# The experts' loop of a two-layer encoder: the next tokens turned between the halves of a first product, the gated activations behind the second product

## The chip, the core and the metric

The kernel runs on one core of a Trainium2 chip. The core has five engines that run beside each other, each through its own queue in order: TensorE (PE, with its weight loads shown as PEld), VectorE (DVE), ScalarE (ACT), GpSimd (POOL) and SyncE (SP, which here only issues loads). The metric is the time of the whole program on the device in microseconds, the median of several runs.

## The reference

The program is an encoder of two layers over 1040 tokens (1024 and 16 learned ones) with 1024 columns. Each layer has a mixer (attention beside a linear recurrence), a layer norm, a mixture of experts, and a layer norm. This case is about the experts: each token is sent to two of 32, and an expert computes

```python
def expert_block(args):
    xe, e = args
    return (jax.nn.silu(xe @ w1[e]) * (xe @ w3[e])) @ w2[e]

yb = lax.map(expert_block, (xb, block_e)).reshape(n_rows, D)
y = jnp.zeros((T, D), jnp.float32).at[row_tok].add(yb.astype(jnp.float32) * row_gate[:, None])
```

`w1` and `w3` are 1024 x 256 each, `w2` is 256 x 1024, all of them float32.

## The kernel before

`moe_layer` (L1180) is called once a layer. It keeps 96 places (`CAP`) for each of the 32 experts (`NE`); what doesn't fit goes through a branch that runs only where an expert has more. Products are made of two parts a number: `high` (L1215, ACT) rounds a weight to the type that PE multiplies fast, `low` (L1219, DVE) takes what is left over, and `mm3` makes three matmuls of each product: high by high, high by low, low by high. `split` does the same for activations, its high part on ACT and its low part on DVE.

The 3 MB of an expert come as thirds (`raw`, 128 x 2048 each): two hold `w1` and `w3` side by side, one for each half of the 1024 rows, and the last holds `w2`. Six `raw` buffers stand in three pools. SP issues a load as soon as the buffer's last reader, a `low`, is done. `w` has six buffers of a high and a low part.

For an expert the loop does:

- `tokens` (L1284): POOL gathers 96 rows into `xs`, of which there are two.
- `turned` (L1230): PE transposes the rows in eight pieces into two `tp` tiles; ACT and DVE split them into `xT`.
- `first` (L1386), halves 0 and 1: 12 matmuls each of `xT` by a third of the weights into `ph`. All 24 go into one PSUM bank.
- `tanh` (L1395, ACT) and `gate` (L1399, two instructions on DVE) make the gated activations `th`.
- `upright` (L1253): PE transposes `th` in two pieces into one `tp` tile; ACT and DVE split it into `aT`.
- `product` (L1261): 12 matmuls by the last third into `py`, two PSUM banks.
- `stored` (L1269): ACT scales `py` by the tokens' gates in two halves into `y`, and POOL scatters its rows (L1273).

`tp` has two buffers, taken in turn by the two tiles of `turned` and the one of `upright`. In PSUM, `tp`, `ph` and `py` fill all eight banks.

The loop runs under `manual_schedule`, so each engine's queue holds the instructions in the order of the code. Round e turns the activations of e, makes the first product of e + 1 and the second of e, prepares the weights of e + 2, turns the tokens of e + 2, and asks for the tokens and the weights of e + 4. The mixers outside are ordered by a scheduler that sees the whole program.

Of the kernel before, what the change touches and what calls it, by code (L numbers as in the profile page):

```python
# [11 lines left out]
F32 = mybir.dt.float32  # L12
# [3 lines left out]
AF = mybir.ActivationFunctionType  # L16
# [5 lines left out]
DEPTH, D, SEQ, META = 2, 1024, 1024, 16  # L22
# [12 lines left out]
NE = 32  # L35
EMPTY = 8192
CAP = 96
# [103 lines left out]
def pool(tc, **kw):  # L141
    return tc.tile_pool(reuse_waits="tile", **kw)
# [12 lines left out]
def pair(pool, shape, name, **kw):  # L155
    return Pair(pool.tile(shape, F32R, name=name + "_hi", **kw), pool.tile(shape, F32R, name=name + "_lo", **kw))
# [14 lines left out]
def hybrid_encoder(ctx: ExitStack, tc: tile.TileContext, I, out):  # L171
# [184 lines left out]
    for li in range(DEPTH):  # L356
# [650 lines left out]
        with mix, ExitStack() as late, pool(tc, name="opp", bufs=2, space=PSUM) as pp, \  # L1007
# [14 lines left out]
            for q, (i, n, col) in enumerate(tiles):  # L1022
# [38 lines left out]
                if len(batch) == size:  # L1061
                    route(op_, batch, lg, lambda: pt_.tile([128, 512], F32, name="pt"))
                    batch = []
            route.tables(op_)
        moe_layer(tc, I, li, last, K, split, mm3, moe, rt, route, h_rows[2 * li + 1], y_dst, nt, dram)
        moe.close()
    combine(DEPTH - 1, None, None)
# [112 lines left out]
def moe_layer(tc, I, li, last, K, split, mm3, stack, rt, route, h1_rows, y_rows, nt, dram):  # L1180
    nc = tc.nc
    ident = K("ident")
    n_rows = nt * 128 if last else L
    V = nc.vector
    VS, XS, GS, M, rk, cnt = route.VS, route.XS, route.at[:, 1], route.M, route.rk, route.cnt
# [4 lines left out]
    def space(name, bufs=1):  # L1190
        return stack.enter_context(pool(tc, name=name + str(li), bufs=bufs))
# [3 lines left out]
    wk, ra = space("moa", 2), space("mob", 2)  # L1195
    wx, ov = space("mox", 2), space("ov")
    rc, ww, rb = (stack.enter_context(pool(tc, name=f"mo{x}{li}", bufs=k, side="right"))
                  for x, k in (("c", 2), ("w", 6), ("d", 2)))
    with pool(tc, name="mop", bufs=1, space=PSUM) as pp:
        xs = [wk.tile([128, D], F32, name=f"xs{q}", bufs=1) for q in range(2)]  # L1200
# [4 lines left out]
        def loaded(src, spaces=(ra, rc, rb)):  # L1205

            r = []
            for q in range(3):
                raw = spaces[thirds[0] // 2 % len(spaces)].tile([128, 2048], F32, name="raw")
                thirds[0] += 1  # L1210
                nc.sync.dma_start(raw, src(q))
                r.append(raw)
            return r

        def high(raw, w, c):  # L1215
            cs = slice(c * 512, (c + 1) * 512)
            nc.scalar.activation(w.hi[:, cs], raw[:, cs], AF.Copy)  # L1217

        def low(raw, w, c):  # L1219
            cs = slice(c * 512, (c + 1) * 512)  # L1220
            V.tensor_tensor(w.lo[:, cs], raw[:, cs], w.hi[:, cs].bitcast(F32), op=OP.subtract)  # L1221

        def third(raw):
            w = pair(ww, [128, 2048], "w")
            for c in range(4):
                high(raw, w, c)
                low(raw, w, c)
            return w

        def turned(x, n):  # L1230
            xT = pair(wx, [128, 8, 128], "xT")[:, :, :n]
            for q in range(2):
                tp = pp.tile([128, 4, 128], F32, name="tp", bufs=2)
                for c in range(4):
                    nc.tensor.transpose(tp[:, c, :n], x[:n, (4 * q + c) * 128:(4 * q + c + 1) * 128], ident[:n, :n])
                split(xT[:, 4 * q:4 * q + 4], tp[:, :, :n])
            return xT
# [15 lines left out]
        def upright(th, n):  # L1253
            tp = pp.tile([128, 4, 128], F32, name="tp", bufs=2)
            for c in range(2):
                nc.tensor.transpose(tp[:, c, :n], th[:, c * 128:(c + 1) * 128], ident[:n, :n])
            aT = pair(wx, [128, 2, 128], "aT")[:, :, :n]
            split(aT, tp[:, 0:2, :n])
            return aT

        def product(aT, w, n):  # L1261
            py = pp.tile([128, D], F32, name="py", bufs=2)
            for j in range(2):
                for c in range(2):
                    mm3(py[:n, j * 512:(j + 1) * 512], aT[:, c], w[:, c * D + j * 512:c * D + (j + 1) * 512],
                        start=c == 0, stop=c == 1)
            return py

        def stored(py, n, vs, gs, rows):  # L1269
            y = wk.tile([128, D], F32, name="y")  # L1270
            for j in range(2):
                nc.scalar.activation(y[:n, j * 512:(j + 1) * 512], py[:n, j * 512:(j + 1) * 512], AF.Copy, scale=gs)  # L1272
            nc.gpsimd.indirect_dma_start(out=rows, out_offset=bass.IndirectOffsetOnAxis(ap=vs, axis=0), in_=y[:n],  # L1273
                                         in_offset=None, bounds_check=2 * n_rows - 1, oob_is_err=False)

        def gather(x, src, xi, rows):
            return nc.gpsimd.indirect_dma_start(out=x, out_offset=None, in_=src[:],
                                                in_offset=bass.IndirectOffsetOnAxis(ap=xi, axis=0),
                                                bounds_check=rows - 1, oob_is_err=False)

        def of(e):
            return loaded(lambda q: I["w_moe"][li, e, :, q * 2048:(q + 1) * 2048])

        def tokens(e):  # L1284
            return gather(xs[e % 2][:CAP], h1_rows, XS[:CAP, e:e + 1], n_rows)


        views = dram_disjoint_views(y_rows[:], NE)
# [85 lines left out]
        raws = [of(0), of(1)]  # L1374
# [4 lines left out]
        with tc.issue_after(route.act.ins), tc.issue_after(route.dve.ins), tc.issue_after(known.ins), tc.issue_after(second.ins):  # L1379
            ws = {0: [third(raws[0][q]) for q in range(2)]}  # L1380
# [3 lines left out]
        phs, ths, xTs = {}, {}, {}  # L1384

        def first(e, half):  # L1386
            if half == 0:
                phs[e] = pp.tile([128, 512], F32, name="ph", bufs=2)
            hidden(phs[e], ws[e][half], xTs[e], CAP, half)

        def portion(e, q):
            if e < NE:
                ws.setdefault(e, []).append(third(raws[e][q]))

        def tanh(e):  # L1395
            ths[e] = wk.tile([128, 256], F32, name="th")[:CAP]
            nc.scalar.activation(ths[e], phs[e][:CAP, :256], AF.Tanh, scale=0.5)

        def gate(e):  # L1399
            th, ph = ths[e], phs.pop(e)  # L1400
            V.scalar_tensor_tensor(th, th, 1.0, ph[:CAP, :256], op0=OP.add, op1=OP.mult)
            V.scalar_tensor_tensor(th, th, 0.5, ph[:CAP, 256:], op0=OP.mult, op1=OP.mult)

        with tc.manual_schedule():
            xTs[0] = turned(xs[0], CAP)
            first(0, 0)
            tokens(2)
            first(0, 1)
            tanh(0)
            gate(0)  # L1410
            xTs[1] = turned(xs[1], CAP)
            tokens(3)
            portion(0, 2)
            raws.append(of(2))
            for q in range(3):
                portion(1, q)
            raws.append(of(3))
            for e in range(NE):
                more, new = e + 1 < NE, e + 2 < NE
                aT = upright(ths.pop(e), CAP)  # L1420
                if more:
                    first(e + 1, 0)
                portion(e + 2, 0)
                if more:
                    first(e + 1, 1)
                portion(e + 2, 1)
                if new:
                    raw, w = raws[e + 2][2], pair(ww, [128, 2048], "w")
                    ws[e + 2].append(w)
                    high(raw, w, 0)  # L1430
                if more:
                    tanh(e + 1)
                    gate(e + 1)
                py = product(aT, ws.pop(e)[2], CAP)
                if new:
                    for c in range(4):
                        if c:
                            high(raw, w, c)
                        low(raw, w, c)
                    if e + 4 < NE:  # L1440
                        raws.append(of(e + 4))
                stored(py, CAP, VS[:CAP, e:e + 1], GS[:CAP, e:e + 1], views[e])
                if new:
                    xTs[e + 2] = turned(xs[e % 2], CAP)
                    if e + 4 < NE:
                        tokens(e + 4)


def rwkv(tc, li, last, K, P, pc, kr_d, bk_d, bon_d, g_dram, vt_d, yT, mhalf, kept, side, ready):
# [326 lines left out]
```

## Time and profile before

| what | value |
|---|---|
| median of 3 runs | 3237.86 us (3231.32 to 3243.92) |
| profiled execution, its own time | 3243.99 us |
| span of the profiled execution | 3242.1 us |
| PE busy | 2737.0 us, 84% |
| DVE busy | 2174.9 us, 67% |
| ACT busy | 1658.0 us, 51% |
| POOL busy | 1040.8 us, 32% |
| low parts of the experts' weights, DVE L1221 | 768, 472.8 us |
| high parts of the experts' weights, ACT L1217 | 768, 412.1 us |

The expert loops are the two stretches in which the memory queues are at nine tenths in the page's second part: about 1223 to 1580 us and 2821 to 3184 us of the span. A busy share over the whole span says little about them; what an expert costs is read inside these stretches. In rows of a timeline the first number is the start, the second the time until the last of the merged instructions ends, and in brackets stands the idle time before with what ended it. An instruction's time there includes what the next one overlaps, so where many follow each other their cost is the distance of the starts.

### The profile page before, as it was taken

The numbers are of one execution on the slowest core, as the hardware profiler recorded it, in microseconds if no ns is written. First come the engines' busy times: TensorE is split into PE (matmuls) and PEld (weight loads), VectorE is DVE, ScalarE is ACT, GpSimd is POOL, SyncE is SP. The second block draws the span as 40 slices with busy tenths as digits, with TensorE's granted clock in tenths as the row PEclk, the third lists the DMA queues.
The fourth block names the chain that finished last, engine by engine and source line by source line (L and its number), as shares of the span: only waits on it lengthen the run. The fifth ranks groups of instructions, "written<-read, shape, count | busy, mean of one in ns | idle before, by whom it ended". The sixth has DMA issues, their size and how long they took to land. (4 is left out here: it accounts for less than half of the span.)

```text
span 3242.1 us, 57910 instructions
## 1 busy us (share of the span) xinstructions
PE 2737.0 (84%) x22160; PEld 2231.9 (69%) x22160; DVE 2174.9 (67%) x4257; ACT 1658.0 (51%) x3604; POOL 1040.8 (32%) x1049
## 2 busy tenths in 40 slices
PE   5989899979998978888498997999699889788882
PEld 4878687768776765666388876888587767566551
DVE  7667554566677668888656747445666666787885
ACT  5334454544445447777433435445344434577772
POOL 3656211143336411111245632112433544111111
PEclk9999899968978979999799988988787879799996
DMA  5345610233323449999724565102432325688875
GB/s 175 103 144 174 200 35 21 66 108 105 91 78 96 144 176 327 323 318 314 252 70 136 161 205 182 40 14 75 130 101 67 95 81 185 235 310 313 309 278 223
DMA packets 342732, 523.76 MB, mean 162 GB/s; under 512 B 110733, under 2 KB 263309, under 8 KB 315809
## 3 DMA queue, kind: packets, MB, share of 16 engines
q1 hardware_dynamic: 234832, 399.11, 38.2%
q10 hardware_dynamic: 93280, 87.04, 7.9%
q0 software_dynamic: 14336, 33.84, 2.9%
q8 instruction: 176, 2.88, 0.4%
q14 instruction: 108, 0.88, 0.1%
HBM read 406.57 MB, written 129.84 MB: 165 GB/s over the span
## 5 line engine op out<-in xcount | busy, mean ns | idle before, releaser
L1221 DVE TENSOR_TENSOR w_lo<-raw,w_hi 128x512 fp32r<-128x512 f32 x768 | 472.8, 684 | 9.3 <-ACT w_hi L1217 9.1
L1217 ACT ACTIVATE w_hi<-raw 128x512 fp32r<-128x512 f32 x768 | 412.1, 620 | 0.0
L201 PE MATMUL pj<-hT_hi,w_hi 128*128 128x352 f32 (+1 forms) x912 | 303.3, 333 | 3.7 <-ACT k L437 2.7
L202 PE MATMUL pj<-hT_lo,w_hi 128*128 128x352 f32 (+1 forms) x912 | 301.4, 331 | 2.8 <-DVE hT_lo L212 2.8
L203 PE MATMUL pj<-hT_hi,w_lo 128*128 128x352 f32 (+1 forms) x912 | 299.7, 329 | 0.0
L1273 POOL DMA_INDIRECT y_rows<-y,VS x64 | 64.5, 1007 | 617.6 <-ACT y L1272 595.7
L201 PE MATMUL ph<-w_hi,xT_hi 128*96 128x512 f32 x512 | 226.9, 443 | 3.4 <-ACT w_hi L1217 3.4
L202 PE MATMUL ph<-w_lo,xT_hi 128*96 128x512 f32 x512 | 222.7, 435 | 1.3 <-DVE w_lo L1221 1.3
L203 PE MATMUL ph<-w_hi,xT_lo 128*96 128x512 f32 x512 | 221.4, 432 | 0.0
L1509 PE MATMUL e<-T,BK 64*128 64x128 f32 x1072 | 171.8, 340 | 38.3 <-DMA T<-kr_d 21.0
L212 DVE TENSOR_TENSOR pT_lo<-tr,pT_hi 128x512 fp32r<-128x512 f32 (+2 forms) x176 | 101.4, 592 | 127.5 <-ACT pT_hi L209 127.0
L201 PEld LDWEIGHTS pj<-hT_hi,w_hi 128*128 128x128 f32 x912 | 176.6, 194 | 14.6 <-issue 6.9
L202 PEld LDWEIGHTS pj<-hT_lo,w_hi 128*128 128x128 f32 x912 | 176.6, 194 | 9.3 <-issue 4.9
L1509 PEld LDWEIGHTS e<-T,BK 64*128 64x128 f32 x1072 | 145.0, 234 | 54.1 <-ACT AA L1515 19.8
L203 PEld LDWEIGHTS pj<-hT_hi,w_lo 128*128 128x128 f32 x912 | 176.1, 193 | 5.0 <-issue 4.3
L1514 DVE TENSOR_TENSOR T<-e,cc 64x512 f32<-64x512 f32 x134 | 92.2, 688 | 89.3 <-PE e L1509 86.9
L1654 POOL TENSOR_TENSOR sp<-ring,pc 64x256 f32<-64x256 f32 x126 | 85.2, 676 | 165.9 <-DVE ring L1667 145.1
L209 ACT ACTIVATE pT_hi<-tr 128x512 fp32r<-128x512 f32 (+2 forms) x176 | 86.7, 517 | 94.3 <-PE tr L873 92.9
L1551 DVE TENSOR_TENSOR sb<-sb,dg 128x16 f32<-128x16 f32 (+8 forms) x270 | 107.1, 397 | 40.5 <-POOL dg L1543 33.4
L203 PEld LDWEIGHTS ph<-w_hi,xT_lo 128*96 128x96 f32 x512 | 93.1, 182 | 43.1 <-issue 3.2
L201 PEld LDWEIGHTS ph<-w_hi,xT_hi 128*96 128x96 f32 x512 | 93.4, 182 | 42.5 <-ACT w_hi L1217 4.1
L202 PEld LDWEIGHTS ph<-w_lo,xT_hi 128*96 128x96 f32 x512 | 93.1, 182 | 40.2 <-DVE w_lo L1221 2.3
(422 smaller groups left out, 7635.3 us busy)
## 6 DMA issues: line engine op xcount, KB each, us to landing
raw<-in_w_moe_dram SPq DMA_DIRECT2D x192, 1024.0 KB
w_raw<-in_w_in_dram SPq DMA_DIRECT2D x38, 512.0 KB
T<-kr_d SPq DMA_DIRECT2D x134, 128.0 KB
ys<-y_rows SPq DMA_DIRECT2D x16, 1024.0 KB
a_d<-ht SPq DMA_DIRECT2D x25, 512.0 KB
h_rows<-h ACTq DMA_DIRECT2D x24, 512.0 KB
kr_d<-KR ACTq DMA_DIRECT2D x16, 576.0 KB
bk_d<-BK ACTq DMA_DIRECT2D x16, 576.0 KB
```

Of the source, the lines that this page charges most:

```text
L201: nc.tensor.matmul(o, a.hi, b.hi, start=start, stop=False)
L202: nc.tensor.matmul(o, a.hi, b.lo, start=False, stop=False)
L203: nc.tensor.matmul(o, a.lo, b.hi, start=False, stop=stop)
L209: hi = nc.scalar.activation(dst.hi, src, AF.Copy)
L212: return hi, e_lo.tensor_tensor(dst.lo, src, dst.hi.bitcast(F32), op=OP.subtract)
L1217: nc.scalar.activation(w.hi[:, cs], raw[:, cs], AF.Copy)
L1221: V.tensor_tensor(w.lo[:, cs], raw[:, cs], w.hi[:, cs].bitcast(F32), op=OP.subtract)
L1273: nc.gpsimd.indirect_dma_start(out=rows, out_offset=bass.IndirectOffsetOnAxis(ap=vs, axis=0), in_=y[:n], in_offset=None, bounds_check=2 * ...
L1509: nc.tensor.matmul(ps[o][:, u], BK[h, q0 + u].rearrange("p a t -> p (a t)"), T[h, q0 + u, o], start=True, stop=True)
L1514: V.tensor_tensor(T[b, q, o], ps[o][b], mask[b, None, :].to_broadcast([64, 4, 128]), op=OP.mult)
L1551: V.tensor_tensor(sb[:, :, cs], sb[:, :, cs], dg[:, :, t_:t_ + 1].to_broadcast([128, n, w]), op=OP.mult)
L1654: nc.gpsimd.tensor_tensor(sp[a], ring[a, :, o], pc[a, d, :, c:c + 1].to_broadcast([64, 4, 64]), op=OP.mult)
```

## The change

The arithmetic, the tiles and the buffers stay as they are. In a round of the loop three things move:

- `turned` for e + 2, with its gather for e + 4, moves from the end of the round to between the two halves of the first product of e + 1.
- `upright` for e + 1 moves from the start of the next round to directly behind the second product of e. On ACT its high part stands between the two halves of the scaling.
- The weights of e + 2 are prepared in a finer order: the first third at the start, the middle third behind `turned` with its last low part after the gate, the first two pieces of `w2` before the scaling, the last two after it.

The scaling gets its own helper, `scaled`, and the scatter stands in the loop.

```diff
+        def scaled(y, py, e, j):
+            nc.scalar.activation(y[:CAP, j * 512:(j + 1) * 512], py[:CAP, j * 512:(j + 1) * 512], AF.Copy,
+                                 scale=GS[:CAP, e:e + 1])
+
         with tc.manual_schedule():
...
+            aT = upright(ths.pop(0), CAP)
             for q in range(3):
                 portion(1, q)
             raws.append(of(3))
             for e in range(NE):
                 more, new = e + 1 < NE, e + 2 < NE
-                aT = upright(ths.pop(e), CAP)
                 if more:
                     first(e + 1, 0)
                 portion(e + 2, 0)
+                if new:
+
+                    xTs[e + 2] = turned(xs[e % 2], CAP)
+                    if e + 4 < NE:
+                        tokens(e + 4)
                 if more:
                     first(e + 1, 1)
-                portion(e + 2, 1)
                 if new:
-                    raw, w = raws[e + 2][2], pair(ww, [128, 2048], "w")
-                    ws[e + 2].append(w)
-                    high(raw, w, 0)
+                    mid, w1 = raws[e + 2][1], pair(ww, [128, 2048], "w")
+                    ws[e + 2].append(w1)
+                    for c in range(4):
+                        high(mid, w1, c)
+                        if c < 3:
+                            low(mid, w1, c)
                 if more:
                     tanh(e + 1)
                     gate(e + 1)
                 py = product(aT, ws.pop(e)[2], CAP)
+                y = wk.tile([128, D], F32, name="y")
                 if new:
-                    for c in range(4):
-                        if c:
-                            high(raw, w, c)
+                    low(mid, w1, 3)
+                    raw, w = raws[e + 2][2], pair(ww, [128, 2048], "w")
+                    ws[e + 2].append(w)
+                    for c in range(2):
+                        high(raw, w, c)
+                        low(raw, w, c)
+                scaled(y, py, e, 0)
+                if more:
+                    aT = upright(ths.pop(e + 1), CAP)
+                scaled(y, py, e, 1)
+                nc.gpsimd.indirect_dma_start(out=views[e], out_offset=bass.IndirectOffsetOnAxis(ap=VS[:CAP, e:e + 1], axis=0),
+                                             in_=y[:CAP], in_offset=None, bounds_check=2 * n_rows - 1, oob_is_err=False)
+                if new:
+                    for c in range(2, 4):
+                        high(raw, w, c)
                         low(raw, w, c)
                     if e + 4 < NE:
                         raws.append(of(e + 4))
-                stored(py, CAP, VS[:CAP, e:e + 1], GS[:CAP, e:e + 1], views[e])
-                if new:
-                    xTs[e + 2] = turned(xs[e % 2], CAP)
-                    if e + 4 < NE:
-                        tokens(e + 4)
```

The order in which the instructions stand shows the move on three engines. First PE, before, at the end of a second product in the middle of the loop (`py` is the second product, `xs` the tokens, `th` the gated activations, `ph` the first product):

```order
L201 MATMUL py<-w_hi,aT_hi 96x512
L202 MATMUL py<-w_lo,aT_hi 96x512
L203 MATMUL py<-w_hi,aT_lo 96x512
L1235 MATMUL tp<-cc,xs_12507 128x96 x8
L1256 MATMUL tp<-cc,th 128x96 x2
```

PE of the changed kernel, in the middle of a first product:

```order
L201 MATMUL ph<-w_hi,xT_hi 96x512
L202 MATMUL ph<-w_lo,xT_hi 96x512
L203 MATMUL ph<-w_hi,xT_lo 96x512
L1235 MATMUL tp<-cc,xs_12507 128x96 x8
L201 MATMUL ph<-w_hi,xT_hi 96x512
L202 MATMUL ph<-w_lo,xT_hi 96x512
L203 MATMUL ph<-w_hi,xT_lo 96x512
```

The eight transposes of the tokens have moved between matmuls of the first product, and the two of the activations follow the second product alone.

ACT before, one round from `tanh` to `tanh`:

```order
L1397 ACTIVATE th<-ph 96x256
L1217 ACTIVATE w_hi<-raw 128x512 x3
L1272 ACTIVATE y<-py,at 96x512 x2
L209 ACTIVATE xT_hi<-tp 128x4x96 x2
L209 ACTIVATE aT_hi<-tp 128x2x96
L1217 ACTIVATE w_hi<-raw 128x512 x9
```

ACT of the changed kernel, one round:

```order
L1397 ACTIVATE th<-ph 96x256
L1217 ACTIVATE w_hi<-raw 128x512 x2
L1405 ACTIVATE y<-py,at 96x512
L209 ACTIVATE aT_hi<-tp 128x2x96
L1405 ACTIVATE y<-py,at 96x512
L1217 ACTIVATE w_hi<-raw 128x512 x6
L209 ACTIVATE xT_hi<-tp 128x4x96 x2
L1217 ACTIVATE w_hi<-raw 128x512 x4
```

The high part of the activations has moved between the two scalings, and that of the tokens away from them, between weights.

DVE before, one round from the gate to the next:

```order
L1401 SCALAR_TENSOR_TENSOR th<-th,ph 96x256
L1402 SCALAR_TENSOR_TENSOR th<-th,ph 96x256
L1221 TENSOR_TENSOR w_lo<-raw,w_hi 128x512 x4
L212 TENSOR_TENSOR xT_lo<-tp,xT_hi 128x4x96 x2
L212 TENSOR_TENSOR aT_lo<-tp,aT_hi 128x2x96
L1221 TENSOR_TENSOR w_lo<-raw,w_hi 128x512 x8
```

DVE of the changed kernel, one round:

```order
L1401 SCALAR_TENSOR_TENSOR th<-th,ph 96x256
L1402 SCALAR_TENSOR_TENSOR th<-th,ph 96x256
L1221 TENSOR_TENSOR w_lo<-raw,w_hi 128x512 x3
L212 TENSOR_TENSOR aT_lo<-tp,aT_hi 128x2x96
L1221 TENSOR_TENSOR w_lo<-raw,w_hi 128x512 x6
L212 TENSOR_TENSOR xT_lo<-tp,xT_hi 128x4x96 x2
L1221 TENSOR_TENSOR w_lo<-raw,w_hi 128x512 x3
```

The tokens' low parts now stand in the middle of the weights, and three low parts of the middle third stand between them and the gate.

## The prediction

> **What bounds the kernel now.** The page's slices show two stretches of five slices with the memory queues at nine tenths; they are the two expert loops. I therefore read POOL's timeline first: POOL sends each expert's result away (L1273), so the starts of these rows are the loop's clock. First, thirtieth, thirty-first and last expert of layer 0, then of layer 1:
>
> ```profile
> 1223.23 3.22 POOL L1273 DMA_INDIRECT y_rows<-y,VS  x1 [15.87 <-ACT y L1272]
> ...
> 1564.67 0.93 POOL L1273 DMA_INDIRECT y_rows<-y,VS  x1 [11.63 <-ACT y L1272]
> 1575.70 0.91 POOL L1273 DMA_INDIRECT y_rows<-y,VS  x1 [10.11 <-ACT aT_hi L209]
> 1580.34 0.91 POOL L1273 DMA_INDIRECT y_rows<-y,VS  x1 [3.72 <-ACT y L1272]
> ...
> 2821.29 3.24 POOL L1273 DMA_INDIRECT y_rows<-y,VS  x1 [15.86 <-ACT y L1272]
> ...
> 3166.74 0.93 POOL L1273 DMA_INDIRECT y_rows<-y,VS  x1 [10.17 <-ACT y L1272]
> 3179.43 0.91 POOL L1273 DMA_INDIRECT y_rows<-y,VS  x1 [11.76 <-ACT aT_hi L209]
> 3184.07 0.91 POOL L1273 DMA_INDIRECT y_rows<-y,VS  x1 [3.73 <-ACT y L1272]
> ```
>
> From first to thirtieth are 29 steps: 341.44 us in layer 0 (1564.67 - 1223.23) and 345.45 us in layer 1. The 58 steps take 686.9 us, 11.84 each. What an expert needs of each engine stands in the view by windows; the first row covers 26 experts, the next two one expert each:
>
> ```profile
> 1249.00:1552.00 303.00, 260.06 (x1196) 183.25 (x1196) 247.79 (x442) 232.99 (x469) 49.51 (x52) 0.94 0.91 316
> ...
> 1237.96:1248.95 10.99, 9.33 (x46) 6.65 (x46) 9.53 (x17) 8.97 (x20) 1.91 (x3) 1.00 0.93 307
> 1248.95:1261.52 12.57, 10.91 (x46) 7.61 (x46) 9.53 (x17) 8.97 (x20) 1.91 (x3) 0.86 0.92 329
> ```
>
> Columns: stretch, its length, then PE, PEld, DVE, ACT, POOL busy, granted clock, memory queues' share, GB/s. 303 / 26 = 11.65 us an expert, while PE needs 9.33 at full clock, DVE 9.53 and ACT 8.97. No engine is full, so waits set the pace. An expert takes 10.99 us at clock 1.00, or 12.57 when a half-clock stretch falls in: 1.58 more. The list of waits for the same 303 us names the wait on PE, and one expert on PE shows where it lies:
>
> ```profile
> PE tp L1256 <- DVE xT_lo L212: 43.1, 26, 1.7
> ...
> 1285.82 0.38 PE L1256 MATMUL tp<-cc,th 96*128 96x96 f32 x2 [1.66 <-DVE xT_lo L212]
> 1285.99 0.46 PE L201 MATMUL ph<-w_hi,xT_hi 128*96 128x512 f32 x1
> ...
> 1291.57 0.39 PE L201 MATMUL py<-w_hi,aT_hi 128*96 128x512 f32 x1
> ...
> 1294.33 0.82 PE L1235 MATMUL tp<-cc,xs 96*128 96x96 f32 x8
> ...
> 1296.81 0.39 PE L1256 MATMUL tp<-cc,th 96*128 96x96 f32 x2 [1.66 <-DVE xT_lo L212]
> 1296.98 0.46 PE L201 MATMUL ph<-w_hi,xT_hi 128*96 128x512 f32 x1
> ```
>
> PE's order is: turn the gated activations (`upright`, 0.17 us to the next row), 24 matmuls of the first product (5.58), 12 of the second (2.76), turn the next tokens (`turned`, 0.82), and wait 1.66. The wait is for a PSUM buffer: `tp` has two, `turned` fills both, and `upright` can have one only when ACT and DVE have split it. ACT does this last, behind two `y` scalings that themselves wait for the second product.
>
> The half-clock stretches hang on the same place. The same view for the `ph` matmuls alone, cut into 3.41 us pieces:
>
> ```profile
> 1294.49:1297.90 3.41, 0.92 (x4) 0.73 (x5) 0.00 (x0) 0.00 (x0) 1.00 0.93 356
> 1297.90:1301.31 3.41, 3.41 (x9) 2.22 (x8) 0.00 (x0) 0.00 (x0) 0.50 0.83 285
> 1318.38:1321.79 3.41, 1.25 (x6) 0.93 (x7) 0.00 (x0) 0.00 (x0) 1.00 0.99 384
> 1321.79:1325.20 3.41, 3.41 (x16) 2.39 (x15) 0.00 (x0) 0.00 (x0) 1.00 0.84 317
> ```
>
> A piece with 0.92 us of product matmuls is followed by a piece at clock 0.50; one with 1.25 us is not. The stretch without them (1294.33 to 1296.98, 2.65 us, transposes included) costs 1.66 in every expert, and another 1.58 in those where nearly all of it falls into one piece.
>
> **The change, step by step.** It removes and adds no arithmetic; only orders move. Durations on ACT and DVE come from these rows, one expert of ACT, and a run of DVE at the loop's start in which it never pauses:
>
> ```profile
> 1286.24 0.33 ACT L209 ACTIVATE aT_hi<-tp 128x192 fp32r<-128x192 f32 x1 [0.69 <-PE tp L1256]
> 1286.47 4.79 ACT L1217 ACTIVATE w_hi<-raw 128x512 fp32r<-128x512 f32 x9
> 1294.53 1.26 ACT L1272 ACTIVATE y<-py,at 96x512 f32<-96x512 f32 x2 [0.82 <-PE py L203]
> 1295.69 0.86 ACT L209 ACTIVATE xT_hi<-tp 128x384 fp32r<-128x384 f32 x2
> ...
> 1287.12 4.91 DVE L1221 TENSOR_TENSOR w_lo<-raw,w_hi 128x512 fp32r<-128x512 f32 x8 [0.16 <-ACT w_hi L1217]
> ...
> 1217.27 0.35 DVE L212 TENSOR_TENSOR aT_lo<-tp,aT_hi 128x192 fp32r<-128x192 f32 x1
> 1217.54 4.89 DVE L1221 TENSOR_TENSOR w_lo<-raw,w_hi 128x512 fp32r<-128x512 f32 x8
> 1222.36 0.41 DVE L1401 SCALAR_TENSOR_TENSOR th<-th,ph 96x256 f32<-96x256 f32 x1
> 1222.80 0.42 DVE L1402 SCALAR_TENSOR_TENSOR th<-th,ph 96x256 f32<-96x256 f32 x1
> 1223.13 2.49 DVE L1221 TENSOR_TENSOR w_lo<-raw,w_hi 128x512 fp32r<-128x512 f32 x4
> 1225.54 1.01 DVE L212 TENSOR_TENSOR xT_lo<-tp,xT_hi 128x384 fp32r<-128x384 f32 x2
> ```
>
> *PE.* `turned` now stands between the halves of the first product, `upright` right behind the second. PE alone: 0.17 + 5.58 + 0.82 + 2.76 = 9.33 us an expert. `upright` now waits for two things: its `tp` buffer, whose reader finished half an expert ago, and the gate on DVE. The second tile of `turned` needs the buffer of the last `upright`, asked for 3.4 us after that (0.17 + 2.8 + 0.4); DVE reaches `aT_lo` about 2 us after it (below). Neither stalls PE.
>
> *The circle of waits.* Put `upright` at 0. The second product ends at 9.33. ACT starts `y` 0.20 later (1294.33 to 1294.53), at 9.53; a scaling takes 0.58 (two to the next row: 1.16), so `aT_hi` starts at 10.11, the second `y` at 10.33 (0.23 later), the third high part of w2 at 10.91. Its low part on DVE starts 0.65 later (1286.47 to 1287.12), at 11.56. Behind it DVE has six low parts at 0.60 (4.82 for eight, 1217.54 to 1222.36), two `xT_lo` (1.01), three low parts of the middle third (1.81) and the gate (0.86, 1222.36 to 1223.22): 7.30 us, to 18.86. The next but one `upright` follows, say at 18.9. That is two periods: 9.45 us each. Ahead of that low part DVE does one middle part, two w2 parts and `aT_lo`, some 2.4 us from the gate, which just fits.
>
> *DVE and ACT.* DVE's whole work for an expert, without a pause, is 9.28 us by the run above (1217.27 to 1226.55). ACT needs 8.97. Both lie below 9.45.
>
> *The token fetch.* POOL's gather for e+4 moves ahead of the store of y(e); it starts when `turned` is done, some 6 us earlier in the expert, and its data are wanted almost two experts later. Nothing queues behind it but that store. Cost: nothing. *SP* still issues three loads an expert, each when DVE frees a buffer.
>
> *Clock.* Without the 1.66 wait no 3.41 us piece holds more than about 0.82 + 0.17 + 0.1 us without product matmuls, far from the 2.5 of the piece above. The half clock should go from the loop.
>
> *Memory.* An expert moves 316 GB/s x 303 us / 26 = 3.68 MB. Two stretches of 20 us at the loops' starts hold the same mix, with DVE nearly always busy (19.2 of 20 us), and one of 7 us only weights:
>
> ```profile
> 1215.00:1222.00 7.00, 7.00 (x34) 4.89 (x33) 7.00 (x13) 7.00 (x16) 0.00 (x0) 0.93 1.01 425
> 1212.00:1232.00 20.00, 15.97 (x61) 10.95 (x61) 19.27 (x35) 16.71 (x34) 4.20 (x2) 0.82 0.99 385
> 2810.50:2830.50 20.00, 15.77 (x63) 10.86 (x63) 19.23 (x35) 16.27 (x34) 4.22 (x2) 0.84 0.99 382
> ```
>
> 3.68 MB at 383 GB/s is 9.6 us. The bounds: 9.45 by the circle if the queues do better, and 10.6 if the 303 us are the measure (316 GB/s at a share of 0.91 is 347 at 1.00; 3.68 / 0.347). The Trainium skill ("DMA: Bandwidth & Descriptors", Where 436 GB/s comes from) speaks against the change here: it puts what one core gets from its memory at about 358 GB/s, by which an expert could not go below 10.3 us. The 425 and 385 above, of a core alone on its chip, disagree. I take **9.6 us**, the value of the rows with the same mix.
>
> *Start and end.* The store of y(0) now waits for `upright(1)`, which stands behind `xT_lo` on DVE: about 2 us later. The two last experts turn no tokens. The thirtieth to thirty-first step becomes 0.17 + 5.58 + 2.76 = 8.5 us; the last about 3.8 (now 4.64, less the `aT_hi` that no longer waits for both `y`). Together 12.3 for 15.67 and 17.33.
>
> *The rest.* The second layer's mixer (1585 to 2757) is ordered by a scheduler and comes out slightly rearranged. I take nothing, with 17 us to both sides: so much do the two layers' stages ahead of the experts differ.
>
> ```profile
> 1585.00:2757.00 1172.00, 1015.96 (x9251) 868.10 (x9252) 730.05 (x1400) 508.95 (x1135) 445.42 (x447) 0.86 0.38 116
> 0.00:1155.00 1155.00, 1015.47 (x9570) 860.65 (x9571) 746.97 (x1453) 534.32 (x1203) 448.72 (x460) 0.91 0.37 112
> ```
>
> *Sum.* Layer 0: 341.4 - 29 x 9.6 - 2 = 61.0, end 3.4. Layer 1: 345.45 - 278.4 - 2 = 65.0, end 5.0. Together 134 us. The profiled execution took 3243.99 us, so 3110 by it; the median of three was 6.1 lower, 3237.86, so **3104 us** against that.
>
> **The rivals.**
>
> *Memory sets the pace at 10.6 us.* For it: a share of 0.91 over 303 us, with bursts of weights, stores and gathers on the same queues. Against it: the 385 and 382. 58 x 1.0 = 58 us more: 3162. By the page's 358 GB/s (10.3 us) it would be 3144. Chance 0.17.
>
> *The half clock stays, whatever the gap.* Then each expert keeps the mean loss of 0.65 (11.65 - 11.0): 9.6 + 0.65 = 10.25, 38 us more: 3142. Against it: the four pieces above. The Trainium skill ("TensorE: Matmul & The Clock Gate", Why this matters for your kernels) warns only of idle gaps over about 3 us between bursts; by that rule the gap of 2.65 costs no clock today, and its going saves none. The rows disagree: the clock fell behind a piece with 2.49 us free of products. Its Part 4 says that transposes do not count as busy, and the rows agree: only so do 0.92 and 1.25 part the two cases. Chance 0.08.
>
> *The wait only moves.* The gate comes late on DVE by what was won, since three low parts and two `xT_lo` stand ahead of it, and `upright` waits 1.66 and more as before: 3238. From the circle I get under 0.1 us of wait. Chance 0.03.
>
> *Slower: a late gate that also costs the clock.* If the middle third of the weights lands late, ACT holds `tanh` behind it, and `upright` waits. From a wait of about 2.3 us on (2.49 less 0.17) the piece falls under 0.92 us of products again. An expert then takes 9.33 + 2.3 + 0.65 = 12.28, 0.44 over 11.84: 58 x 0.44 = 26 us, 3263. Against it: the high parts, which read `raw`, had no idle time before any of the 768. Chance 0.04.
>
> ```profile
> L1217 ACT ACTIVATE w_hi<-raw 128x512 fp32r<-128x512 f32 x768 | 412.1, 620 | 0.0
> ```
>
> **How the numbers follow.** My forecast (9.4 to 9.9 us an expert, mixer as now) has 0.68. Its likeliest time is 3104. The low end is 9.45 an expert (58 x 0.15 = 9 less) and a mixer faster by about 15: 3080. The high end takes in memory at 10.6 with 8 for the mixer: 3170. Faster by over 0.5% (under 3222, about what a measurement of this kernel can tell from no change): 0.68 + 0.17 + 0.08 = 0.93. Within: 0.03. Slower: 0.04.
>
> **What would show it.** POOL's stores 9.4 to 9.9 us apart, without the 11.0 and 12.6; PE's wait ahead of `upright` under 0.3 us; clock 1.00 throughout the loops; about 380 GB/s there. If ACT's high parts wait for `raw`, memory is the bound. If clock 0.5 pieces remain, the second rival holds. If the 1585 to 2757 stage moves by over 17 us, the scheduler's part is mis-sized.

## The result, and the profile after

The changed kernel takes 3147.85 us (median of 4 runs, 3129.36 to 3161.33), the kernel before 3240.89 us beside it (4 runs, 3231.32 to 3247.85): a ratio of 0.971, 95% interval 0.966 to 0.975. In a second series (run e1 below) it was 0.972, 0.968 to 0.977. The direction and the range of the prediction hold. Its gain of 134 us does not: the medians differ by 93 us, the two profiled executions by 86.0 (3243.99 and 3157.96).

The loop's pace is again read from POOL's timeline, in the changed kernel. First, sixth, thirtieth, thirty-first and last store of layer 0; first, seventh, thirtieth, thirty-first and last of layer 1:

```profile
1232.95 0.96 POOL L1458 DMA_INDIRECT y_rows<-y,VS  x1 [4.40 <-ACT y L1405]
1279.98 0.94 POOL L1458 DMA_INDIRECT y_rows<-y,VS  x1 [5.92 <-ACT y L1405]
1529.37 0.91 POOL L1458 DMA_INDIRECT y_rows<-y,VS  x1 [8.73 <-ACT y L1405]
1537.83 0.91 POOL L1458 DMA_INDIRECT y_rows<-y,VS  x1 [7.55 <-ACT y L1405]
1541.65 0.91 POOL L1458 DMA_INDIRECT y_rows<-y,VS  x1 [2.91 <-ACT y L1405]
2789.72 0.96 POOL L1458 DMA_INDIRECT y_rows<-y,VS  x1 [4.40 <-ACT y L1405]
2846.26 0.93 POOL L1458 DMA_INDIRECT y_rows<-y,VS  x1 [5.61 <-ACT y L1405]
3085.58 0.91 POOL L1458 DMA_INDIRECT y_rows<-y,VS  x1 [8.70 <-ACT y L1405]
3094.21 0.91 POOL L1458 DMA_INDIRECT y_rows<-y,VS  x1 [7.71 <-ACT y L1405]
3098.06 0.91 POOL L1458 DMA_INDIRECT y_rows<-y,VS  x1 [2.94 <-ACT y L1405]
```

29 steps take 296.42 us in layer 0 (before: 341.44) and 295.86 us in layer 1 (before: 345.45), so 45.0 and 49.6 us went. But the loop has two paces: the first five steps take 9.41 us each (47.03 / 5; in layer 1 six of 9.42), the 24 after them 10.39 (249.39 / 24). The view by windows of the changed kernel shows the two paces side by side, with the columns of the prediction (length, PE, PEld, DVE, ACT, POOL busy, clock, DMA share, GB/s):

```profile
1232.95:1279.98 47.03, 46.59 (x233) 32.83 (x232) 46.38 (x87) 43.82 (x91) 11.01 (x11) 1.00 1.01 353
1300.95:1519.70 218.75, 198.34 (x968) 138.95 (x967) 196.54 (x358) 186.13 (x379) 40.95 (x41) 0.98 1.00 356
2857.00:3066.00 209.00, 187.63 (x920) 130.28 (x919) 186.58 (x340) 176.53 (x360) 39.99 (x40) 1.00 1.00 353
```

In the first stretch PE and DVE are nearly full (46.59 and 46.38 of 47.03). It can go faster at the same 353 GB/s because it still uses up loads made ahead: 353 GB/s for 47.03 us are an estimated 3.32 MB for each of its five experts, and the prediction's 3.68 MB is what one needs. In the long ones both have some 10% idle, the clock is 0.98 to 1.00, and the DMA engines are busy throughout at only 353 to 356 GB/s. What PE, ACT and DVE wait for there stands in the list of waits of the changed kernel from 1249 to 1500 us (total, times, longest), and for the whole program in ACT's group of the page:

```profile
ACT w_hi L1217 <- DMA raw<-in_w_moe_dram: 23.1, 26, 2.0
DVE w_lo L1221 <- ACT w_hi L1217: 21.9, 37, 1.9
PE tp L1256 <- DVE th L1402: 21.0, 21, 2.2
...
L1217 ACT ACTIVATE w_hi<-raw 128x512 fp32r<-128x512 f32 x768 | 424.7, 625 | 71.0 <-DMA raw<-in_w_moe_dram 57.3
```

The three waits are one chain: ACT waits for a weight load, DVE for ACT, and PE for the gate on DVE. Before, ACT's group had 0.0 idle; now it waits 57.3 us for `raw`. The weights arrive late: this is the rival of the prediction in which memory sets the pace, from the sixth or seventh step on.

### The profile page after: what moved, and what is told of

It reads as the page before. It is cut to its first block, busy times and chain, and to the rows that moved or that the text cites. A ratio compares the mean times of both kernels' runs of the same rounds, so it can differ in the third digit from the quotient of the medians.

```text
span 3156.2 us, 58039 instructions
## 1 busy us (share of the span) xinstructions
PE 2707.3 (86%) x22160; PEld 2209.1 (70%) x22160; DVE 2165.3 (69%) x4257; ACT 1650.5 (52%) x3604; POOL 1050.7 (33%) x1049
## 5 line engine op out<-in xcount | busy, mean ns | idle before, releaser
L1221 DVE TENSOR_TENSOR w_lo<-raw,w_hi 128x512 fp32r<-128x512 f32 x768 | 481.7, 684 | 49.4 <-ACT w_hi L1217 49.1
L1217 ACT ACTIVATE w_hi<-raw 128x512 fp32r<-128x512 f32 x768 | 424.7, 625 | 71.0 <-DMA raw<-in_w_moe_dram 57.3
L201 PE MATMUL ph<-w_hi,xT_hi 128*96 128x512 f32 x512 | 213.8, 418 | 3.9 <-ACT w_hi L1217 3.9
L202 PE MATMUL ph<-w_lo,xT_hi 128*96 128x512 f32 x512 | 206.0, 402 | 1.4 <-DVE w_lo L1221 1.4
L1528 PE MATMUL e<-T,BK 64*128 64x128 f32 x1072 | 181.0, 352 | 28.5 <-DMA T<-kr_d 19.0
L203 PE MATMUL ph<-w_hi,xT_lo 128*96 128x512 f32 x512 | 205.3, 401 | 0.0
L212 DVE TENSOR_TENSOR pT_lo<-tr,pT_hi 128x512 fp32r<-128x512 f32 (+2 forms) x176 | 101.3, 592 | 130.1 <-ACT pT_hi L209 129.7
L1528 PEld LDWEIGHTS e<-T,BK 64*128 64x128 f32 x1072 | 152.7, 244 | 44.9 <-DMA T<-kr_d 15.6
L1277 POOL DMA_INDIRECT xs<-h_rows,XS x64 | 77.3, 1208 | 159.9 <-PE tp L1235 97.0
L1540 POOL TENSOR_TENSOR AA<-AA,cc 128x256 f32<-128x256 f32 x67 | 52.0, 777 | 221.4 <-ACT AA L1534 161.8
L421 POOL TENSOR_SCALAR w_hi<-w_raw 128x1024 fp32r<-128x1024 f32 x34 | 102.3, 3010 | 59.4 <-PE pj L202 59.4
```

The source lines that it names most:

```text
L201: nc.tensor.matmul(o, a.hi, b.hi, start=start, stop=False)
L202: nc.tensor.matmul(o, a.hi, b.lo, start=False, stop=False)
L203: nc.tensor.matmul(o, a.lo, b.hi, start=False, stop=stop)
L212: return hi, e_lo.tensor_tensor(dst.lo, src, dst.hi.bitcast(F32), op=OP.subtract)
L421: nc.gpsimd.tensor_scalar(w.hi, wr, 1.0, None, op0=OP.mult)
L1528: nc.tensor.matmul(ps[o][:, u], BK[h, q0 + u].rearrange("p a t -> p (a t)"), T[h, q0 + u, o], start=True, stop=True)
```

## The experiments

Two questions were open: why memory gives 10.4 us an expert and not 9.6, and which part of the change brings the gain. All runs in one table; the steps are worked out from the starts of POOL's stores, the paces from the second to the sixth store and from the thirteenth to the twenty-ninth, layer 0 / layer 1:

| run | 29 steps, us | early pace | late pace | time, us |
|---|---|---|---|---|
| before | 341.4 / 345.4 | 11.78 / 11.88 | 11.58 / 11.87 | 3240.89 |
| e1 the change | 296.5 / 296.4 | 9.37 / 9.43 | 10.46 / 10.48 | 3147.98 |
| e2 the change, places spread | 278.3 / 276.1 | 9.38 / 9.42 | 9.69 / 9.60 | 3106.22 |
| e3 before, places spread | 340.7 / 345.3 | 11.38 / 11.49 | 11.58 / 11.87 | 3231.35 |
| e4 the change, two thirds loaded | 273.5 / 273.3 | 9.38 / 9.41 | 9.37 / 9.42 | 3099.03 |
| e5 spread, `turned` put back | 384.8 / 391.4 | 13.39 / 13.53 | 13.38 / 13.45 | 3342.28 |
| e6 spread, `upright` put back | 277.8 / 278.6 | 9.55 / 9.61 | 9.60 / 9.61 | 3119.61 |
| e7 spread, splits put back | 284.6 / 286.1 | 9.81 / 9.83 | 9.81 / 9.81 | 3121.43 |
| e8 before, spread, only `turned` moved | 274.5 / 273.6 | 9.16 / 9.23 | 9.71 / 9.60 | 3107.90 |
| e9 before, only `turned` moved | 293.3 / 292.1 | 9.20 / 9.23 | 10.32 / 10.39 | 3151.28 |
| e10 as e8, timed | 275.3 / 274.7 | 9.16 / 9.23 | 9.70 / 9.69 | 3094.82 |
| e11 the change, spread by halves | 294.3 / 292.7 | 9.38 / 9.42 | 10.33 / 10.33 | 3134.63 |

The times of e3 to e8 and e11 are single executions. Medians of six were taken for e1, e2, e9 and e10. The kernel before, run beside each series, took 3242.59 us (e1 to e4), 3250.73 (e5 to e8, one execution) and 3244.39 (e9 to e11). The stages outside the loops come out up to 18 us apart over these runs (from the last store of layer 0 to the first gather of layer 1: 1208.0 us before, 1200.9 in e3 with the same mixer, 1200.5 in e10, 1218.9 in e5), so the 29 steps tell the cases apart better than the whole.

### e1 and e2: where the token rows lie

The loads' own records gave the idea. Each weight load reports that it is done in 16 parts, as many as there are DMA engines. In the late part of the changed kernel five or six parts came after 5 to 6 us, and the others 8 to 16 us after the issue. 96 places on 16 engines are six places in a row for each; an expert has 65 tokens on the average (2 x 1040 / 32), and these fill the first places. So if engines own runs of six places, 11 of them carry all token rows, and 5 carry none.

e1 is the changed kernel again. e2 gives the tokens other places. The router compares a token's rank with a row of constants, one a place; the edit permutes that row (the row's other reader now takes a row with the same first 16 numbers):

```diff
-    put("iota128", j[None])
+    put("iota128", np.where(j < CAP, j % 6 * 16 + j // 6, j)[None])
...
-        nc.vector.tensor_copy(pf[:, :META], K("iota128")[:, :META])
+        nc.vector.tensor_copy(pf[:, :META], K("iota32")[:, :META])
```

> The changed kernel itself, timed beside the next one. Both theories: as in its first runs, about 3148 us and 0.971 of the kernel before; 29 steps of the experts' stores of 295 to 297 us in each layer, 9.4 us each in the first five or six experts and 10.4 us each after them.

> The changed kernel with the tokens of an expert put into its 96 places in another order: place j takes rank (j mod 6) x 16 + j / 6, so that each run of six places in a row holds about as many tokens as any other; sums and bytes are the same. Theory A (the token rows are served by some of the 16 DMA engines only, those of the first 65 places, and the weights' share on those engines is late): the later experts fall from 10.4 to the circle's 9.4 to 9.6 us, 29 steps to 273 to 280 us in each layer, 33 to 46 us off the whole, about 3102 to 3115 us, 0.957 to 0.961 of the kernel before. Theory B (all engines together give at most about 355 GB/s for this traffic, however it is shared out): the later experts stay at 10.2 to 10.5 us and the time within 5 us of the changed kernel's.

e1: 3147.98 us, ratio 0.972. e2: 3106.22 us, ratio 0.958 (0.953 to 0.963), 29 steps of 278.3 and 276.1 us. The late pace fell from 10.5 to 9.6 or 9.7. The view by windows of e2 for the late part of layer 0, and ACT's group on its page:

```profile
1340.00:1500.00 160.00, 154.46 (x767) 108.54 (x766) 153.86 (x282) 147.62 (x299) 33.65 (x32) 1.00 1.02 384
...
L1217 ACT ACTIVATE w_hi<-raw 128x512 fp32r<-128x512 f32 x768 | 422.6, 627 | 17.0 <-DMA raw<-in_w_moe_dram 12.3
```

The same bytes per expert now go at 384 GB/s in place of 356, and ACT's wait for `raw` falls from 57.3 to 12.3 us. Theory B, a limit of about 355 GB/s for this traffic, is refuted.

### e3: the same places in the kernel before

> The kernel before with the same other order of places. Both theories: its experts take 11.0 and 12.6 us in turn, longer than the traffic by either account, so 29 steps stay at 340 to 346 us and the time within 10 us of 3241.

340.7 and 345.3 us, and 3231.35 us: as before. The places make no difference where the loop is slower (11.6 to 11.9 us an expert) than the late pace of 10.5 us that they set in e1. (It fell within the 10 us expected, but a single time says no more.)

### e4: a third less to load

Experts 2 to 31 load two thirds of their weights, and the second product uses the second third in place of the missing one. The work of PE, ACT and DVE stays the same.

```diff
-            for q in range(3):
+            for q in range(3 if thirds[0] < 6 else 2):
...
-            return r
+            return (r + r[1:])[:3]
```

> The changed kernel, in which experts 2 to 31 load two thirds of their weights, and the second third stands in for the last one (the output is another): 2.63 MB per expert in place of 3.68. If the later experts of the changed kernel wait for memory, by A or by B, all 29 steps go at the circle of waits, 9.4 to 9.5 us each, 273 to 276 us in each layer, some 42 us less over both, about 3105 us. If something else holds them at 10.4 us (PE, DVE, ACT or a wait that grows from expert to expert), they stay at 10.2 to 10.4 us and 295 us.

273.5 and 273.3 us, the late pace as the early one. The view by windows of e4 over the same stretch shows queues with room, and its page no wait at all for `raw`:

```profile
1340.00:1500.00 160.00, 158.28 (x787) 111.38 (x786) 157.23 (x290) 148.37 (x306) 35.03 (x32) 1.00 0.79 260
...
L1217 ACT ACTIVATE w_hi<-raw 128x512 fp32r<-128x512 f32 x768 | 420.3, 629 | 0.0
```

So the late loads alone made the late pace, and 9.37 to 9.42 us is what the changed order gives without it.

### e11: which engines count

e2 changed two things: how many rows the fullest engine has, and the order in which the rows' addresses come. e11 mixes ranks and places as strongly, but within each half of 48 places, so that eight runs of six stay full at 65 tokens:

```diff
-    put("iota128", j[None])
+    put("iota128", np.where(j < CAP, j // 48 * 48 + j % 6 * 8 + j % 48 // 6, j)[None])
```

> The changed kernel with ranks and places mixed within each half of the 96 places only: with 65 tokens, each of the first eight runs of six places still holds six of them, the ninth three and the other seven two each. The order in which rows come is as far from the first one as in the full spread. Theory A1 (the fullest DMA engines set the pace): 10.2 to 10.4 us in the later experts, 29 steps of 290 to 297 us, as in the changed kernel. Theory A2 (what counts is that no engine is left without rows, or the order in which the rows' addresses come): 9.4 to 9.7 us, 29 steps of 274 to 281 us, as with the full spread.

294.3 and 292.7 us, late pace 10.33: theory A1. The records of the loads agree. Medians of when a load's 16 parts report, in us from its issue, over 33 to 40 loads each in the late part of layer 0 (worked out from the trace's semaphore records, sorted):

```
before  4.7  4.7  4.7  4.8  4.8  4.9  5.0  5.0  5.1  5.2  5.2  5.4  5.7  5.9  6.9  7.6
e1      5.2  5.2  5.3  5.3  5.5  6.0  9.1 11.4 11.7 12.1 13.8 14.4 14.7 15.4 15.9 16.5
e11     5.2  5.3  5.3  5.4  5.5  5.5  5.6  5.9 13.5 14.0 14.3 14.5 14.9 15.4 15.9 16.2
e2      6.3  8.1  8.6  8.7  8.8  8.9  9.2  9.4  9.5 10.4 10.9 11.2 11.6 11.8 12.8 14.7
```

In e11 eight parts are early and eight late: just as many as there are full runs of places. In e1 five are early, the sixth and seventh between, in e2 the two groups are gone. A load is usable only when its last part is in: in e1, wherever ACT had to wait for a load, its first instruction on it starts 0.02 to 0.10 us after the sixteenth part (the same records, 1300 to 1500 us).

A rate can be estimated from this. A full run of places carries per expert a sixteenth of the weights (3.146 MB / 16 = 196.6 KB) and six rows fetched and six stored, 4.1 KB each (49.2 KB): 245.8 KB in 10.4 us are 23.6 GB/s for one engine. With the rows spread evenly (130 / 16 rows, 33.3 KB) it would be 229.9 KB, by the same rate 9.7 us. e10 measures 9.69 and 9.70, e2 9.60 and 9.69.

### e5, e6 and e7: one part of the change undone

These three stand on e2, so that memory hides less. e5 puts `turned` and the gather back to the end of the round, behind `upright`:

```diff
-                if new:
-
-                    xTs[e + 2] = turned(xs[e % 2], CAP)
-                    if e + 4 < NE:
-                        tokens(e + 4)
                 if more:
                     first(e + 1, 1)
...
                         raws.append(of(e + 4))
+                    xTs[e + 2] = turned(xs[e % 2], CAP)
+                    if e + 4 < NE:
+                        tokens(e + 4)
```

> The changed kernel with the other order of places (so that memory hides nothing), in which the turning of the tokens stands at the end of the round again, behind the upright turning; the rest of the change stays. Theory (a turning with nothing of the first product behind it makes PE wait for the splits that free its tile): the 9.33 us of PE and a wait of 1.4 to 1.7 us, 10.7 to 11.0 us an expert, or up to 12.6 where the half clock comes back with it: 29 steps 310 to 355 us in place of 276 to 278. Rival (the gain came from the order of the weights' splits and the early store): 9.4 to 10.0 us, 29 steps of 272 to 290 us.

A miss on the bad side: 384.8 and 391.4 us, 13.4 us an expert, and 3342.28 us in all, some 90 more than the kernel before beside it (3250.73; the steps alone are 89 more). PE's timeline in e5, from the end of one second product into the next first product:

```profile
1349.89 0.49 PE L1235 MATMUL tp<-cc,xs 96*128 96x96 f32 x4
1351.27 0.55 PE L1235 MATMUL tp<-cc,xs 96*128 96x96 f32 x4 [0.89 <-DVE aT_lo L212]
1352.87 0.74 PE L201 MATMUL ph<-w_hi,xT_hi 128*96 128x512 f32 x1 [1.04 <-ACT xT_hi L209]
1353.41 0.63 PE L202 MATMUL ph<-w_lo,xT_hi 128*96 128x512 f32 x1
1353.83 0.68 PE L203 MATMUL ph<-w_hi,xT_lo 128*96 128x512 f32 x1
...
1356.38 0.40 PE L203 MATMUL ph<-w_hi,xT_lo 128*96 128x512 f32 x1
1356.61 0.39 PE L201 MATMUL ph<-w_hi,xT_hi 128*96 128x512 f32 x1
```

Two waits in place of one: 0.89 for the `tp` buffer that `upright` held, as expected, and 1.04 more, since the first product now wants the tokens turned a moment ago. The second wait was left out of the expectation. And the half clock follows in nearly every expert: matmuls 0.42 us apart (1353.41 to 1353.83) until 1356.38, then 0.23; eight at the slow distance cost about 1.7 us. Three of the 29 steps in layer 0 go without it and take 11.95 us, most others 13.5: the price of 1.58 that the prediction read from before. Of the 11.95, PE's own 9.2 (e8, below) and the two waits make 11.1. A step at full clock has a third wait of 0.20, for `xT_lo` ahead of the third matmul (at 1341.83). Most of the rest is in the transposes: with a wait behind each group of four they take 0.49 and 0.55, in e8 all eight cost 0.60.

e6 puts `upright` back to the start of the next round:

```diff
                 more, new = e + 1 < NE, e + 2 < NE
+                aT = upright(ths.pop(e), CAP)
...
                 scaled(y, py, e, 0)
-                if more:
-                    aT = upright(ths.pop(e + 1), CAP)
                 scaled(y, py, e, 1)
```

> The changed kernel with the other order of places, in which the upright turning stands at the start of the next round again, so that both halves of y and the last two splits of w2 come ahead of aT's. PE's own order is the same. Theory (PE has 6 us until it needs aT, and the second tile of the tokens' turning is freed in time): 9.4 to 9.7 us an expert, 29 steps of 275 to 283 us. Rival (aT's splits, now behind four more operations of ACT, free the tile late, and PE waits for it ahead of every second tile): 10.0 us or more, 290 us or more.

e6: 277.8 and 278.6 us, 9.55 to 9.61 a step, as the theory had it; the place of `upright` is worth 0.2 us a step where memory does not bind.

e7 splits the whole middle third and the first piece of w2 ahead of `tanh`, as before:

```diff
-                    mid, w1 = raws[e + 2][1], pair(ww, [128, 2048], "w")
-                    ws[e + 2].append(w1)
-                    for c in range(4):
-                        high(mid, w1, c)
-                        if c < 3:
-                            low(mid, w1, c)
+                    portion(e + 2, 1)
+                    raw, w = raws[e + 2][2], pair(ww, [128, 2048], "w")
+                    ws[e + 2].append(w)
+                    high(raw, w, 0)
...
-                    low(mid, w1, 3)
-                    raw, w = raws[e + 2][2], pair(ww, [128, 2048], "w")
-                    ws[e + 2].append(w)
                     for c in range(2):
-                        high(raw, w, c)
+                        if c:
+                            high(raw, w, c)
                         low(raw, w, c)
```

> The changed kernel with the other order of places, in which the last low part of w1 and the first high part of w2 stand ahead of tanh and gate again, as before. Theory of the circle (gate sits in it, and the two operations come ahead of it): each step 0.3 to 0.6 us longer, 9.7 to 10.0 us, 29 steps of 282 to 291 us. Rival (PE alone sets the 9.4 us and gate has slack): 9.4 to 9.5 us, 274 to 280 us.

9.81 us in nearly every step, 0.4 over e2's early pace, inside the 0.3 to 0.6 that the circle of waits foretold.

### e8, e9 and e10: one part alone

e8 is the kernel before with the spread places and a single move, that of `turned` with its gather; e9 is the same with the places as they were, e10 is e8 timed.

```diff
                 portion(e + 2, 0)
+                if new:
+                    xTs[e + 2] = turned(xs[e % 2], CAP)
+                    if e + 4 < NE:
+                        tokens(e + 4)
                 if more:
                     first(e + 1, 1)
...
-                if new:
-                    xTs[e + 2] = turned(xs[e % 2], CAP)
-                    if e + 4 < NE:
-                        tokens(e + 4)
```

> The kernel before with the other order of places and the tokens' turning, with its gather, between the halves of the next first product, and nothing else of the change. Theory (the place of that turning is what costs before): 9.4 to 9.9 us an expert, 29 steps of 273 to 288 us. Rival (the upright turning and the order of the splits are needed as well): 10.3 us or more, 300 us or more.

> The kernel before with the tokens' turning, and its gather, between the halves of the next first product, and nothing else: the places are as before. Theory (this move is the whole gain; then the token rows on 11 of the 16 DMA engines bind): 9.2 us in the first experts, about 10.2 to 10.4 us after them, 29 steps of 293 to 297 us, about 3150 us, 0.969 to 0.975 of the kernel before. Rival (the other parts of the change help once memory binds): 29 steps of 300 us or more, 0.976 or more.

> The same with the tokens spread over the 96 places, timed (its single look gave 3107.9 us and 29 steps of 274.5 and 273.6 us). Theory: with the rows on all engines memory binds only late in the loops, so its time is that of the whole change with spread places within 0.4%: 3098 to 3112 us, 0.955 to 0.961 of the kernel before. Rival (the upright turning behind the second product and the later splits of w2 are worth something still): 3115 us or more.

e8: 274.5 and 273.6 us. e9: 3151.28 us, ratio 0.970 (0.966 to 0.973), the same as the whole change (0.972, 0.968 to 0.977). e10: 3094.82 us, a little below the range expected, ratio 0.952 (0.948 to 0.956): the best of all, though its interval overlaps that of e2. So the one move, `turned` with its gather, is the whole gain in time within these intervals (no run moved the gather alone). Its early pace is even below that of the whole change. The view by windows of e8, 80 us early in layer 0:

```profile
1240.00:1320.00 80.00, 80.00 (x404) 56.76 (x403) 79.69 (x149) 76.07 (x158) 26.10 (x17) 1.00 1.02 381
```

PE has no gap in 80 us: 9.2 us an expert is PE itself, with DVE close behind (79.69 of 80). The 9.33 of the prediction was a little high, since `turned` costs 0.60 to the next row where a product follows at once (1282.30 to 1282.90 in e8), not 0.82. In the changed kernel the last two parts of w2 stand behind the scaling of `y` on ACT, and so behind the second product; that closes the circle through DVE and the gate and makes 9.4. In e8 ACT makes all parts of w2 ahead of `y`, so the circle is not there. (That it is this edge was argued from the order; no run moved it alone.)

## Why the prediction came out as it did

*Right: the wait and its price.* PE's wait of 1.66 us ahead of `upright` is gone in the early steps, and with it nearly all of the half clock, which the prediction expected to go "from the loop". In the 58 steps before, 27 stretches of 3.41 us ran at clock 0.50; in the changed kernel it is two, both in the late part of layer 0 (hence the 0.98 of that window), and they have another cause (below, the late gate). PE in the changed kernel, two `upright` rows an expert apart in the early part and one in the late part:

```profile
1259.34 0.36 PE L1256 MATMUL tp<-cc,th 96*128 96x96 f32 x2
1268.87 0.36 PE L1256 MATMUL tp<-cc,th 96*128 96x96 f32 x2 [0.22 <-DVE th L1402]
...
1351.82 0.36 PE L1256 MATMUL tp<-cc,th 96*128 96x96 f32 x2 [1.10 <-DVE th L1402]
```

0.22 is inside the 0.3 foretold. The 1.10 later on is the gate held up by the weights. The rival of a half clock that stays whatever the gap fell with this, and so did the wait that only moves.

*Right: the circle.* 9.45 us foretold, 9.37 to 9.43 measured wherever memory did not bind (e1 early, e4 throughout), and e7 lengthened it by 0.4. The steps show its form too: the prediction's circle closes over two experts in 18.9 us, and in layer 0 of e4 the steps alternate between 9.53 and 9.21, 18.74 for two. What the prediction did not see is that the order of the change itself seems to make this circle (argued, as said under e8), and that with `turned` moved alone the steps reach PE's own 9.2.

*Right: start and ends.* From the first gather to the first store 2 us more were foretold; it is 1.9 in both layers (33.34 to 35.21 us, and 32.97 to 34.87). The end was to be 12.3 us; it is 12.28 and 12.48 (1541.65 - 1529.37, 3098.06 - 3085.58).

*Wrong: the size of the memory term, and the rate taken for it.* "3.68 MB at 383 GB/s is 9.6 us" was the size chosen, from "two stretches of 20 us at the loops' starts" that were said to "hold the same mix". They do not. The views of the DMA queues, of the kernel before for one of those stretches and for its 303 us, and of the changed kernel for its late part (packets, MB, share of 16 engines; q0 carries the token rows):

```profile
q0 software_dynamic: 203, 0.44, 5.7%
...
q0 software_dynamic: 5824, 13.92, 12.8%
...
q1 hardware_dynamic: 9218, 66.78, 84.8%
q0 software_dynamic: 4609, 10.98, 14.5%
```

At the loop's start the rows had 5.7% of the engines' time, in the loop 12.8 and 14.5%: the stretch held two stores or gathers of POOL (the x2 of its row in the prediction), where 20 us of the loop at 9.6 us would have four. The queue's row for the stretch would have shown it. But the better mix alone would not have given the answer, because the sum over all engines was the wrong quantity: 384 GB/s were to be had (e2), and still the kernel got 356, since a load waits for the fullest engine. Steps of 10.2 us on the average in place of 9.6 account for 35.5 of the 48 us by which the two profiled executions fall short (predicted 686.9 - 58 x 9.6 = 130.1, measured 45.0 + 49.6 = 94.6).

*The rest of the miss: 13.1 us outside the loops*, inside the 17 allowed. Ahead of the first loop the profiled execution is 7.85 us longer with the same instructions in the same order on each engine, and the stage between the loops 5.2. e1, the same kernel, has 0.7 and 2.2 there, so this differs from run to run.

*The rival that came true in part.* "Memory sets the pace at 10.6 us", 3162, had a chance of 0.17. Its figure for the pace was right within 0.2 us for the late part of the loop, and 3162 is nearer to the 3147.85 than 3104 is. It was held unlikely for the sake of the same two stretches. So the time lies inside the range only because the range took in this rival (up to 3170): the case that the prediction gave 0.68, 9.4 to 9.9 us an expert, did not come about, with 10.2 on the average. The late loop ran at 353 to 356 GB/s. The Trainium skill ("DMA: Bandwidth & Descriptors", Where 436 GB/s comes from) gives about 358 GB/s as a core's share. The figure fits and the reason does not: e2 moved the same bytes per expert at 384.

*Slower, by a late gate.* The weights did land late and the gate did hold `upright`, mostly by about 1 us (1.10 in the row above). In two experts of layer 0 it held it by 1.96 and 2.20 us (to 1393.89 and 1465.81), and both times 3.41 us at clock 0.50 followed. So a wait shorter than the 2.3 us that the prediction worked out is enough, and the `ph` matmuls of a piece do not alone decide: 1.29 us of them in the piece ahead of 1394.05 were followed by the half clock, and in the prediction's rows 1.25 were not. What decides between two such pieces stays open. By the price of 1.7 us seen in e5 the two cost some 3 us. e1 has two such stretches as well, in layer 1, behind waits of 1.96 and 1.95 us; the loops of e2 and e4, in which ACT waits 12.3 us and not at all for `raw`, have none from their second store on. e5 shows what such a gap costs once it is there in every expert: some 90 us more than before.

## What to carry to other kernels

A stretch that is to stand for a loop's memory rate has to hold the same share of each queue, not only a busy DMA row. Where rows are gathered or scattered beside large loads, count what the fullest DMA engine carries, since each load waits for its last part: here a permutation of one row of constants was worth another 42 us (3147.98 to 3106.22). And when a change has several parts, run each alone: one move, eight transposes and the gather behind them, carried the whole gain, and the reordering around it cost 0.2 us an expert until memory hid that.

## What the runs showed of the hardware

- In a gather or scatter of 96 rows, six places in a row seem to go to one DMA engine, and rows that are left out (places without a token) leave their engine idle: five or six of a load's 16 parts were early where five engines had no rows on the average, eight where eight had few. With the same bytes the late pace was 10.3 to 10.5 us with runs of six full, and 9.6 to 9.7 us with about four rows an engine.
- By this reading one loaded engine went at an estimated 23.6 GB/s under this mix (245.8 KB in 10.4 us), while a stretch of 7 us with only weights had 425 GB/s, 26.6 an engine.
- The half clock falls in nearly every expert in e5, whose turnings and two waits hold the products back for 3.15 us (1349.72, where `upright` starts, to 1352.87), against 2.65 us before, where only part of the experts had it. In the changed kernel the products stood still for 2.26 us once (1391.77 to 1394.03, all of it in one piece of 3.41 us), and that was enough.
